# Attention logits as three half-height products, two heads in the two row halves of TensorE

## The chip, the cores and the metric

The kernel runs on one core of a Trainium2 chip. The metric is device time in microseconds from the first to the last instruction of the program on that core. Three runs of the kernel before gave 1956.97, 1957.89 and 1959.04 us; their median is 1957.89 us.

## The reference: what is computed

The input `x` is one sequence of 2048 positions of width 1024. It is normalised and multiplied by one wide input matrix, which yields the queries, keys and values of two attention mixers, gate paths and merge gates. All of it is fp32.

- Mixer A: 8 query heads share 2 key/value heads, head width 64, and each position looks at the 128 positions on either side of it. Each head has a sink logit.
- Mixer B: three groups of 8 heads, head width 64. Each group is a windowed attention on every first, fourth or sixteenth position, with 64 neighbours on either side. The groups are combined by their softmax denominators.

What the change touches is the step from the queries and keys to the logits:

```python
qa = head_rms_norm(qa.reshape(bsz, S, A_Q_HEADS, HEAD_DIM), q_norm_a[layer]) * scale
ka = head_rms_norm(ka.reshape(bsz, S, A_KV_HEADS, HEAD_DIM), k_norm_a[layer])
...
scores = jnp.einsum('bnqkgd,bnmkd->bkgnqm', qb, kw).astype(jnp.float32)
...
logits = jnp.where(valid, scores + bias, NEG_INF)
```

After the mixers, both outputs are gated, projected, merged by sigmoid gates, projected once more and added to `x`.

## The kernel before, in words

**Split numbers.** Matmuls run on fp16 operands. An fp32 value is stored as a high fp16 part and a low fp16 part (the rest), and a product is summed from several matmuls of parts into one fp32 accumulator. A projection uses three: high by high, high by low, low by high.

**Stages.** A first stage loads, normalises, transposes and splits `x` into `XH` and `XL`. The attention stage works through 14 units: 2 units of mixer A (4 query heads and their one key/value head each) and 12 of mixer B (a pair of heads of one group each). A last stage does the merge gates, the branch projections and the output projection.

**A unit.** A unit's positions are cut into 16 subsets of 128 positions, handled two at a time by class `Pair`, so there are 8 pairs for each unit. `Pair.matmuls` (line 651) projects a subset's queries, keys and values into a PSUM tile `pj`. `Pair.plan` then queues the steps `square`, `stats`, `newton`, `scale`, `gain`, `hi`, `lo`, `swap` and `turn`: the head norms on VectorE and GpSimd, and the split into the fp16 tile `spl`. `hi` (line 728, ScalarE) writes the high parts, `lo` (line 732, VectorE) the low parts. In `spl` a head's high part of 64 columns lies beside its low part, so that one head fills a block of 128 columns. `swap` (line 737, GpSimd) writes a further block for each key head, with low and high exchanged. `turn` (line 745) issues one DMA transpose for each subset from the SP queue; it gives the tile `kq`, six blocks of 128 rows by 128 positions. The rows of a block are the high and the low part of one head.

**An item.** Class `Item` holds one block of 128 queries and two heads: 256 items in all. `logits` (line 805) multiplies the query block with each key block, once as it is and once with its halves exchanged, so two matmuls of 128 rows give all four products of parts. An item has up to three key blocks in A (12 matmuls for two heads), two in B's first two groups (8) and one in the third (4). The logits stand in PSUM tiles `s` from a pool of three (`s_p`): an A item takes two tiles, one for each head, and a B item takes one tile with both heads beside each other. `maxima` (line 820, VectorE) adds the bias and takes the maximum, `exps` (line 828) and `hi` (line 833) run on ScalarE, `lo` (line 837) on VectorE, `turn` (line 843) transposes the probabilities by DMA into `pt`, and `values` (line 854) multiplies them with the values on TensorE.

**Order.** The order on every engine is written out by the kernel: `at(t, f)` puts a step on a heap of due times, and `until` calls what is due between the projections' matmuls. The offsets in `NORM` and `LAGS` set how long after its pair or item a step is issued. A step's matmuls are issued in one piece, so an item's logits stand as one burst between projection matmuls (lines 308 and 651) or matmuls of line 854. Waits between engines come from the tiles that the steps share.

Of the kernel before, what the change touches and what calls it, by code (L numbers as in the profile page):

```python
# [21 lines left out]
F32 = mybir.dt.float32  # L22
F16 = mybir.dt.float16
I32 = mybir.dt.int32
AF = mybir.ActivationFunctionType
OP = mybir.AluOpType
# [8 lines left out]
HD = 64  # L35
# [76 lines left out]
def block_kernel(tc, x, w_units, w_gate, w_mrg, w_brn, w_out, w_bra, gain, qkg, sink, bias_a, bias_b, b_merge, out):  # L112
    nc = tc.nc
    V = nc.vector
    A = nc.scalar
    G = nc.gpsimd
    T = nc.tensor
# [171 lines left out]
    s_p = main.enter_context(tc.tile_pool(name="sp", bufs=3, space=PSUM))  # L289
# [222 lines left out]
    def scale_time(t):  # L512
        return X_CH[0] + X_CH[1] * t
# [6 lines left out]
    for t in range(NT):  # L520
        b = X_SQ[0] + X_SQ[1] * t if t < 4 else X_SQ[2] + X_SQ[3] * (t - 4)
# [4 lines left out]
        b = scale_time(t)  # L526
        at(b, x_scale, t)
        for h in range(2):
            b = scale_time(t) + X_CH[2] + X_CH[5] * h
# [8 lines left out]
    for c in range(3):  # L538
        b = X_G[c]
# [34 lines left out]
    wk = main.enter_context(tc.tile_pool(name="wk", bufs=2, reuse_waits="tile"))  # L574
# [59 lines left out]
    class Pair:  # L634
# [7 lines left out]
        def matmuls(self, i):  # L642
            un, (r, c) = self.un, self.subsets[i]
            self.ps[i] = ps = pj_p.tile([128, 512], F32, name="pj")
            out = []
            for a, b, aligned in ((0, 128, True), (128, 384, False)) if un.shift else ((0, 384, True),):
                h, lo = subset(0, un.g, r, c, aligned), subset(1, un.g, r, c, aligned)
                k = 0
                for ch in range(NCH):
                    for lhs, rhs in ((h, un.wh), (h, un.wl), (lo, un.wh)):  # L650
                        out.append(lambda lhs=lhs, rhs=rhs, ch=ch, a=a, b=b, k=k: T.matmul(  # L651
                            ps[:, a:b], lhsT=lhs[:, ch, :], rhs=rhs[:, ch, a:b], start=(k == 0), stop=(k == 23)))
                        k += 1
            return out
# [38 lines left out]

        def square(self):
            n = 2 * self.nh * HD
            self.sp = wk.tile([128, 2, 6, 2, HD], F16, name="spl")
            self.sq = self.sp[:].rearrange("p a b c d -> p (a b c d)").bitcast(F32)
            A.activation(self.sq[:, :n], self.rw[:, :n], AF.Square)

        def stats(self):  # L700
# [23 lines left out]
        def hi(self):  # L724

            n = 2 * self.nh
            self.q = self.rw[:, :n * HD].rearrange("p (s h e) -> p s h e", s=2, e=HD)
            A.activation(self.sp[:, :, :self.nh, 0, :], self.q, AF.Copy)  # L728

        def lo(self):  # L730
            sp, nh = self.sp, self.nh
            V.tensor_tensor(sp[:, :, :nh, 1, :], self.q, sp[:, :, :nh, 0, :], OP.subtract)  # L732

        def swap(self):
            sp, nh, nq = self.sp, self.nh, self.un.nq
            for i in range(2):
                G.tensor_copy(sp[:, i, nh:, :, :], sp[:, i, nq:nh, ::-1, :])  # L737

        def turn(self):
            for i, s in enumerate(self.subsets):  # L740
                if self.un.shift and s[1] == 0:
                    kq = wk.tile([128, 6, 128], F16, name="kq0", bufs=3)
                else:
                    kq = wk.tile([128, 6, 128], F16, name="kq", bufs=KQ_BUFS)
                nc.sync.dma_start_transpose(out=kq[:], in_=self.sp[:, i].rearrange("p a b c -> p (a b c)"))
                self.un.kq[s] = kq


    class Item:
# [40 lines left out]
        def logits(self):  # L790
            un = self.un
            q = un.kq[(self.r, self.i)]
            if un.kind == "A":
                self.sv = [s_p.tile([128, 512], F32, name="s")[:, :self.W] for _ in range(2)]
            else:
                t = s_p.tile([128, 512], F32, name="s")
                self.sv = [t[:, self.W * j:self.W * j + self.W] for j in range(2)]
            for j in range(2):
                h = self.h0 + j
                kh = 0 if un.kind == "A" else h  # L800
                o = 0
                for s, k0, k1 in self.keys:
                    kt = un.kq[s]
                    for v in range(2):
                        T.matmul(self.sv[j][:, o:o + k1 - k0], lhsT=q[:, h, :],  # L805
                                 rhs=kt[:, un.nq + kh + v * un.nk, k0:k1], start=(v == 0), stop=(v == 1))
                    o += k1 - k0

        def stat(self, j):
            un = self.un  # L810
# [251 lines left out]
    for u in range(NU + 1):  # L1062
        t = 8 * u
# [8 lines left out]
    for c, u, slots in FILLS:  # L1072
# [4 lines left out]
        t = 8 * u  # L1077
# [5 lines left out]
    for k in range(8):  # L1083
        u = 3 + k
        t = 8 * u
# [10 lines left out]
    un, nxt = None, 0.0  # L1096
    t = 0
    while t < NPAIR or heap or any(k >= t for k in fill):
        u, j = divmod(t, 8)
        steps = [(f, args) for f, *args in fill.pop(t, [])]  # L1100
        if u < NU:
            if j == 0:
                un = Unit(u)
# [127 lines left out]
    def split(hi, lo, v, scale):  # L1231
        return (lambda: A.activation(hi, v, AF.Copy, scale=scale[:]),
                lambda: V.scalar_tensor_tensor(lo, v, scale[:], hi, OP.mult, OP.subtract))
# [211 lines left out]
    t = clock[0]  # L1445
# [120 lines left out]
    t = clock[0]  # L1566
# [7 lines left out]
    for k, (i, q) in enumerate(steps):  # L1574
# [3 lines left out]
        p = (i // 2, q % 2)  # L1578
# [168 lines left out]
```

## Time and profile before

| | us |
|---|---|
| median of three runs | 1957.89 (1956.97 to 1959.04) |
| span of the profiled execution | 1958.6 |
| TensorE busy | 1935.7 (17606 matmuls) |
| weight loads busy | 1392.0 |
| VectorE busy | 1377.4 |
| ScalarE busy | 1059.8 |
| GpSimd busy | 956.0 |
| line 805, logits, summed busy time | 150.7 (2016 matmuls) |

The profile lists instructions by line, engine, operation and tile. PE is TensorE's matmul row and PEld its weight loads, DVE is VectorE, ACT ScalarE, POOL GpSimd and SP the engine that issues the DMAs. A row's form, such as `128*128 128x128 f16`, gives the weights' rows and columns, then the output. A matmul's record lasts from its start to its modelled end, and records overlap: the price of a matmul in a full stream is the distance to the next start, not the length of its record. In groups by line, the time behind `|` is busy time and the mean of one in ns, and the time behind the second `|` is the idle time of the engine before them with its releaser. In waits, the three numbers are the total in us, the number of times and the longest.

### The profile page before, as it was taken

To read this page: it belongs to the slowest core of one execution; us is meant where nothing else is said; L and a number is where in the kernel's file an instruction comes from. 1 tells how busy PE (TensorE), PEld (TensorE's weight loads), DVE (VectorE), ACT (ScalarE), POOL (GpSimd) and SP (SyncE) were. 2 spreads that over 40 slices of the span, in tenths; PEclk is the share of its full clock that TensorE was granted. 3 is DMA by queue.
4 is the path that set the end of the run, shared out by engine and by line. 5 is a ranking of instruction groups with operands and counts; after the bars stand their busy time and mean duration, and the time that the engine had idled before them with its cause. 6 is when DMAs were issued, how large, how long until landed. Compare 5 with 4: busy or idle time off the path is not lost.

```text
span 1958.6 us, 48091 instructions
## 1 busy us (share of the span) xinstructions
PE 1935.7 (99%) x17606; PEld 1392.0 (71%) x17606; DVE 1377.4 (70%) x3604; ACT 1059.8 (54%) x2415; POOL 956.0 (49%) x2440
## 2 busy tenths in 40 slices
PE   8999999999999999999999999999999999999999
PEld 5567896677788898888989889899544444444444
DVE  6668777888768776667876878767776757876312
ACT  7457656776565566565666655656534545432100
POOL 4254556455546656647566676656511210232533
PEclk8999999999999999999999999999999999999999
DMA  6239987797848596677777776755822346788763
GB/s 250 81 81 168 194 150 159 141 187 141 177 101 184 118 185 126 125 148 164 152 132 154 135 169 126 143 118 118 187 81 85 106 165 195 218 241 268 252 228 145
DMA packets 589773, 308.46 MB, mean 157 GB/s; under 512 B 458080, under 2 KB 527328, under 8 KB 588256
## 3 DMA queue, kind: packets, MB, share of 16 engines
q1 hardware_dynamic: 589536, 305.39, 67.0%
q8 instruction: 137, 2.24, 0.5%
q14 instruction: 100, 0.82, 0.1%
HBM read 129.91 MB, written 65.27 MB: 100 GB/s over the span
## 4 chain that ended last, share of the span: by engine, by line
PE 80%; DVE 6%; POOL 6%; issue 4%; ACT 2%; DMA 2%; SPq 0%; POOLq 0%; DVEq 0%; ACTq 0%
PE pj L651 32%; PE pj L308 14%; PE fps L308 13%; PE fps L1614 7%; PE fps L1409 5%; PE s L805 4%; PE pv L854 4%; POOL rs_t L270 1%; DVE rw L715 1%; POOL rs_t L271 1%; DVE qss L703 1%; POOL rs_t L272 1%; POOL rw L722 1%; POOL rs_y L273 1%; PE pt L916 1%
## 5 line engine op out<-in xcount | busy, mean ns | idle before, releaser
L651 PE MATMUL pj<-wl,XH 128*128 128x128 f16 (+2 forms) x2816 | 715.2, 268 | 0.0
L651 PE MATMUL pj<-wh,XH 128*128 128x128 f16 (+2 forms) x2816 | 708.7, 268 | 4.0 <-DVE vt L691 4.0
L651 PE MATMUL pj<-wh,XL 128*128 128x128 f16 (+2 forms) x2816 | 711.6, 269 | 0.0
L651 PEld LDWEIGHTS <-XH 128*128 128x128 f16 x5632 | 574.6, 113 | 64.7 <-issue 5.8
L651 PEld LDWEIGHTS <-XL 128*128 128x128 f16 x2816 | 318.1, 113 | 26.7 <-issue 0.5
L820 DVE CUSTOM_DVE_ANT_0 pr<-s,b,ubuf 128x256 f32<-128x256 f32 (+3 forms) x512 | 218.6, 464 | 48.6 <-PE s L805 47.0
L270 POOL TENSOR_TENSOR rs_t<-rs_y 128x8 f32<-128x8 f32 (+2 forms) x345 | 105.4, 306 | 207.5 <-DVE rs_y L261 142.7
L837 DVE SCALAR_TENSOR_TENSOR p<-pr,p 128x512 f16<-128x512 f32 (+2 forms) x256 | 185.0, 723 | 21.6 <-ACT p L833 21.1
L308 PEld LDWEIGHTS <-wh 128*128 128x128 f16 x960 | 93.7, 98 | 111.0 <-issue 1.5
L715 DVE TENSOR_TENSOR rw<-rw,qr 128x512 f32<-128x512 f32 (+1 forms) x112 | 111.6, 997 | 86.7 <-POOL vt L678 58.4
L722 POOL TENSOR_TENSOR rw<-rw,g 128x128 f32<-128x128 f32 (+1 forms) x224 | 131.1, 605 | 78.1 <-DVE rw L715 62.1
L833 ACT ACTIVATE p<-pr 128x512 f16<-128x512 f32 (+2 forms) x256 | 159.5, 623 | 7.1 <-issue 0.3
L670 ACT ACTIVATE rw<-pj 128x256 f32<-128x256 f32 (+1 forms) x224 | 86.5, 386 | 134.3 <-PE pj L651 133.4
L737 POOL COPY spl<-spl 128x256 f16<-128x256 f16 (+1 forms) x224 | 93.7, 448 | 127.2 <-DVE spl L732 125.7
L308 PE MATMUL fps<-Y,wh 128*128 128x512 f16 x512 | 152.2, 379 | 0.0
L805 PE MATMUL s<-kq 128*128 128x128 f16 (+1 forms) x1856 | 147.3, 218 | 1.5 <-DMA kq<-spl 1.4
L805 PEld LDWEIGHTS <-kq 128*128 128x128 f16 x2016 | 129.8, 98 | 25.1 <-issue 2.0
L308 PE MATMUL pj<-XH,gh 128*128 128x512 f16 x384 | 145.5, 379 | 0.0
L308 PE MATMUL pj<-XH,gl 128*128 128x512 f16 x384 | 145.5, 379 | 0.0
L308 PE MATMUL pj<-XL,gh 128*128 128x512 f16 x384 | 145.5, 379 | 0.0
L1614 PE MATMUL fps<-wt,M 128*128 128x512 f16 (+1 forms) x684 | 145.2, 375 | 0.0
L728 ACT ACTIVATE spl<-rw 128x512 f16<-128x512 f32 (+1 forms) x112 | 72.1, 644 | 126.2 <-POOL vt L678 87.0
(241 smaller groups left out, 3702.2 us busy)
## 6 DMA issues: line engine op xcount, KB each, us to landing
wraw<-in_w_units_dram SPq DMA_DIRECT2D x56, 384.0 KB, 4.6
mtd<-mm SPq DMA_DIRECT2D x56, 256.0 KB, 3.7
M<-mtd SPq DMA_DIRECT2D x8, 1792.0 KB, 9.5
mgd<-fg SPq DMA_DIRECT2D x39, 256.0 KB, 2.1
zd<-z SPq DMA_DIRECT2D x128, 66.0 KB, 1.9
zz<-zd SPq DMA_DIRECT2D x64, 132.0 KB, 2.9
xt<-in_x_dram SPq DMA_DIRECT2D x16, 512.0 KB, 8.9
gtd<-yo SPq DMA_DIRECT2D x32, 256.0 KB, 2.7
```

The lines of the kernel that those rows point to most:

```text
L270: G.tensor_tensor(tv, yv, yv, OP.mult)
L308: out.append(lambda w=w, xx=xx, ch=ch, i=i: T.matmul(ps[:], lhsT=w[:, ch, c0:c0 + 128], rhs=xx[:, ch, ts], start=(i == 0), stop=(i == n - 1)))
L651: out.append(lambda lhs=lhs, rhs=rhs, ch=ch, a=a, b=b, k=k: T.matmul(ps[:, a:b], lhsT=lhs[:, ch, :], rhs=rhs[:, ch, a:b], start=(k == 0), ...
L715: V.tensor_tensor(q, q, self.rr[:, :n].unsqueeze(2).to_broadcast([128, n, HD]), OP.mult)
L722: G.tensor_tensor(q[:, i, :un.nq, :], q[:, i, :un.nq, :], g, OP.mult)
L737: G.tensor_copy(sp[:, i, nh:, :, :], sp[:, i, nq:nh, ::-1, :])
L805: T.matmul(self.sv[j][:, o:o + k1 - k0], lhsT=q[:, h, :], rhs=kt[:, un.nq + kh + v * un.nk, k0:k1], start=(v == 0), stop=(v == 1))
L820: V.tensor_tensor_reduce(out=self.pv[:, j, self.p0:self.p0 + W], in0=self.sv[j], in1=un.bias[:, self.h0 + j, self.b0:self.b0 + W], scale=I ...
L833: A.activation(self.sp[:, :128 * n], self.pr, AF.Copy, scale=PSC)
L837: V.scalar_tensor_tensor(self.sp[:, 128 * n:], self.pr, PSC, self.sp[:, :128 * n], OP.mult, OP.subtract)
L1409: mm.append(lambda ch=ch, k=k, w=w, i=i: T.matmul(ps[:], lhsT=weight(bl, ch)[w], rhs=xblock(x, ch)[k], start=(i == 0), stop=(i == 11)))
L1614: mm.append(lambda ch=ch, k=k, w=w, i=i: T.matmul(ps[:, :cols.stop - cols.start], lhsT=m[:, a, ch, k, :], rhs=wt[w][:, b, ch, cols], start ...
```

## The change

`spl` and `kq` get another layout, and `logits` another set of products.

- `hi` and `lo` write all high parts of a subset first and then all low parts. A block of 128 columns now holds two heads, 64 columns each, of one kind of part. After the transpose, one head lies in rows 0 to 63 and its partner in rows 64 to 127.
- In B a subset has four blocks (queries high, keys high, queries low, keys low), so the transpose moves four instead of six, and `swap` does nothing. In A there are six blocks, and `swap` copies the single key head next to itself, so that it lies in both halves.
- `logits` makes three products for each head and key block, high by high, high by low and low by high; the product of the two low parts is no longer made. Each is a matmul of 64 rows. The two heads of an item alternate, head 0 in rows 0 to 63 and head 1 in rows 64 to 127.
- Every item, B's too, takes two tiles `s`, one for each head. The pool still has three.

An item's burst has 18 matmuls in A (12 at the ends of the sequence), 12 in B's first two groups and 6 in the third.

```diff
         def square(self):
             n = 2 * self.nh * HD
-            self.sp = wk.tile([128, 2, 6, 2, HD], F16, name="spl")
-            self.sq = self.sp[:].rearrange("p a b c d -> p (a b c d)").bitcast(F32)
+            w = self.nw = 4 if self.un.kind == "B" else 6
+            sp = wk.tile([128, 2 * 2 * 6 * HD], F16, name="spl")
+            self.sp = sp[:, :4 * w * HD].rearrange("p (a b c d) -> p a b c d", a=2, b=2, d=HD)
+            self.sq = sp[:].bitcast(F32)
...
-            A.activation(self.sp[:, :, :self.nh, 0, :], self.q, AF.Copy)
+            A.activation(self.sp[:, :, 0, :self.nh, :], self.q, AF.Copy)
...
-            V.tensor_tensor(sp[:, :, :nh, 1, :], self.q, sp[:, :, :nh, 0, :], OP.subtract)
+            V.tensor_tensor(sp[:, :, 1, :nh, :], self.q, sp[:, :, 0, :nh, :], OP.subtract)
 
         def swap(self):
-            sp, nh, nq = self.sp, self.nh, self.un.nq
-            for i in range(2):
-                G.tensor_copy(sp[:, i, nh:, :, :], sp[:, i, nq:nh, ::-1, :])
+            if self.nw > self.nh:
+                for i in range(2):
+                    G.tensor_copy(self.sp[:, i, :, 5, :], self.sp[:, i, :, 4, :])
...
-                nc.sync.dma_start_transpose(out=kq[:], in_=self.sp[:, i].rearrange("p a b c -> p (a b c)"))
+                nc.sync.dma_start_transpose(out=kq[:, :self.nw, :], in_=self.sp[:, i].rearrange("p a b c -> p (a b c)"))
...
         def logits(self):
             un = self.un
             q = un.kq[(self.r, self.i)]
-            if un.kind == "A":
-                self.sv = [s_p.tile([128, 512], F32, name="s")[:, :self.W] for _ in range(2)]
-            else:
-                t = s_p.tile([128, 512], F32, name="s")
-                self.sv = [t[:, self.W * j:self.W * j + self.W] for j in range(2)]
-            for j in range(2):
-                h = self.h0 + j
-                kh = 0 if un.kind == "A" else h
-                o = 0
-                for s, k0, k1 in self.keys:
-                    kt = un.kq[s]
-                    for v in range(2):
-                        T.matmul(self.sv[j][:, o:o + k1 - k0], lhsT=q[:, h, :],
-                                 rhs=kt[:, un.nq + kh + v * un.nk, k0:k1], start=(v == 0), stop=(v == 1))
-                    o += k1 - k0
+            self.sv = [s_p.tile([128, 512], F32, name="s")[:, :self.W] for _ in range(2)]
+            nb = 3 if un.kind == "A" else 2
+            o = 0
+            for s, k0, k1 in self.keys:
+                kt = un.kq[s]
+                for i, (a, b) in enumerate(((0, 0), (0, 1), (1, 0))):
+                    for j in range(2):
+                        rows = slice(64 * j, 64 * j + 64)
+                        T.matmul(self.sv[j][:, o:o + k1 - k0], lhsT=q[rows, nb * a + (self.h0 + j) // 2, :],
+                                 rhs=kt[rows, nb * b + nb - 1, k0:k1], start=(i == 0), stop=(i == 2))
+                o += k1 - k0
```

## The prediction

> **What bounds the kernel.** I read the page's busy shares, slices and chain, then TensorE's waits, its rows by form, and the order of time around single bursts.
>
> ```profile
> span 1958.6 us, 48091 instructions
> PE 1935.7 (99%) x17606; PEld 1392.0 (71%) x17606; DVE 1377.4 (70%) x3604; ACT 1059.8 (54%) x2415; POOL 956.0 (49%) x2440
> ...
> PE   8999999999999999999999999999999999999999
> ...
> PEclk8999999999999999999999999999999999999999
> ...
> PE 80%; DVE 6%; POOL 6%; issue 4%; ACT 2%; DMA 2%; SPq 0%; POOLq 0%; DVEq 0%; ACTq 0%
> ```
>
> TensorE is busy in every slice after the first, at a full clock, and holds 80% of the chain that ended last. A busy share alone could hide small stalls, so TensorE's waits come next.
>
> ```profile
> PE s L468 <- DVE xt L462: 6.4, 4, 4.7
> PE pj L651 <- DVE vt L691: 4.0, 4, 2.4
> PE pt L194 <- DVE yo L920: 3.0, 1, 3.0
> PE s L805 <- DMA kq<-spl: 1.4, 3, 0.8
> ```
>
> These are the four longest; nothing else keeps TensorE waiting for more than about 1 us in total. So TensorE's stream of slots is the time: a slot that is added is added to the end, and work taken from another engine gives nothing. The logits that the change rewrites all lie in the attention stage:
>
> ```profile
> 110.00:1410.00 1300.00, 1290.96 (x14443) 1080.78 (x14442) 988.22 (x2886) 807.04 (x1987) 767.09 (x2226) 1.00 0.75 148
> ```
> ```profile
> 110.00:1410.00 1300.00, 150.70 (x2016) 129.84 (x2016) 1.00 0.75 148
> ```
>
> The first row is the whole stage (span, then busy time of TensorE, weight load, VectorE, ScalarE, GpSimd); the second is line 805 alone, with all its 2016 matmuls and 2016 weight loads.
>
> **What the logits cost now.** Records overlap, so their busy time isn't their price; the price is the distance from one start to the next.
>
> ```profile
> 400.65 0.83 PE L805 MATMUL s<-kq 128*128 128x128 f16 x12
> 401.32 0.33 PE L651 MATMUL pj<-wl,XH 128*128 128x384 f16 x1
> ...
> 402.27 0.70 PE L854 MATMUL pv<-vt,pt 128*128 128x65 f16 x18
> 402.81 0.32 PE L651 MATMUL pj<-wh,XH 128*128 128x384 f16 x1
> ```
> ```profile
> L805 PE MATMUL s<-kq 128*128 128x128 f16 x1776 | 139.5, 219 | 1.5 <-DMA kq<-spl 1.4
> L805 PE MATMUL s<-kq,kq 128*128 128x128 f16 x80 | 8.9, 220 | 0.0
> L805 PE MATMUL s<-kq,kq 128*128 128x64 f16 x80 | 7.8, 193 | 0.0
> L805 PE MATMUL s<-kq 128*128 128x64 f16 x80 | 7.8, 193 | 0.0
> ```
>
> Twelve logit matmuls of 128 columns take 401.32 - 400.65 = 0.67 us, 56 ns each. Eighteen matmuls of 64 or 65 columns of line 854, each with a new 128x128 weight load, take 0.54 us, 30 ns each: that is the price of a short matmul, and also the fastest rate at which this trace shows weight loads being fed. So now: (1776 + 80) x 56 + 160 x 30 ns = 108.7 us.
>
> **Part 1: three products of half height for two of full height.** Per key block and head there were two matmuls; there are three, 1.5 times as many: 3024, of which 2784 have 128 columns and 240 have 64. All records of before say 128*128, so no row shows a 64-row matmul, nor whether two of them in the two row halves run at once. Bounds:
> - Wholly side by side, a pair takes one slot: half of (2784 x 56 + 240 x 30) = 81.6 us, a gain of 27.1.
> - One after the other, each takes its slot: 163.1 us, a loss of 54.4.
> - Side by side, but fed by weight loads at the 30 ns of line 854: 3024 x 30 = 90.7 us, a gain of 18.0.
>
> I take the third, -18.0: the two heads alternate in the diff, each with its own tile `s` and its own rows, and a weight load precedes each matmul, so the nearest row is the one that is paced by weight loads. The Trainium skill ("TensorE: Matmul & The Clock Gate", Part 3) says that matmuls whose operands lie in different row groups run concurrently, and gives 3.07 times for four tiles of 32 rows with 512 columns; by that alone, at its best of two for one, the time would be 1958.6 - 27.1 = 1931.5. No row here shows it.
>
> **Part 2: the change of height.** Each burst of logits now stands between matmuls of 128 rows, so TensorE goes from 128 rows to 64 and back once for each item. ScalarE's line 833 runs once for each item:
>
> ```profile
> L833 ACT ACTIVATE p<-pr 128x512 f16<-128x512 f32 (+2 forms) x256 | 159.5, 623 | 7.1 <-issue 0.3
> ```
>
> 256 items are 512 changes of height. Neighbours of unlike width and line follow each other now without a gap, but the height never changes, so the price of a change isn't shown. Lower end 0; below nothing is excluded, since a change of height computes nothing and takes nothing away. For the upper end:
>
> ```profile
> 805.62 0.38 PE L308 MATMUL pj<-XH,gl 128*128 128x512 f16 x1
> 805.62 0.43 PEld L805 LDWEIGHTS <-kq 128*128 128x128 f16 x4
> ...
> 805.84 0.39 PE L805 MATMUL s<-kq 128*128 128x128 f16 x4
> ...
> 806.06 0.38 PE L308 MATMUL pj<-XH,gh 128*128 128x512 f16 x1
> ```
> ```profile
> L805 PEld LDWEIGHTS <-kq x2016: 95/98/98, 112.8 to 1409.1; 128*128 128x128 f16 x184
> ```
>
> A logit matmul lasts 219 ns while its successor starts after 56: a tail of 163 ns is hidden under the next. The 512-column one has the same tail (0.38 against 0.22 us). Weight loads are pulled ahead too: the first of the four starts at 805.62, its matmul at 805.84. If a change of height takes both overlaps away, it costs 163 + 98 = 261 ns. Ends 0 and 261, no row nearer to either; I take the middle, 130 ns: 512 x 0.130 = +66.6 us (0 to 133.6).
>
> The Trainium skill ("TensorEngine Tiling (Array Packing)", Tiling Modes) says that changing the tiling mode, not just the tile, drains TensorE. It gives no price. If the drain is the 163 ns tail, it costs 83.5 us instead of 66.6, and the sum below would be 2026. No row of before has a change of mode to hold against it.
>
> Against the 18.0 us of part 1, the point from which the change loses is 18.0 / 512 = 35 ns a change (27.1 / 512 = 53 ns at the best pairing).
>
> **Part 3: two tiles `s` for each B item.** The pool has three. B items used one, and now use two, so the second head's first matmul must wait until VectorE has read the first head of the item before. It is in TensorE's order, so every projection behind it waits as well. I laid each burst against VectorE's line 820 of the tile that it would reuse. Only four of the bursts come too early, the worst here:
>
> ```profile
> 1113.20 0.91 PE L805 MATMUL s<-kq 128*128 128x128 f16 x8
> 1118.27 0.61 PE L805 MATMUL s<-kq 128*128 128x128 f16 x8
> ```
> ```profile
> 1120.59 0.47 DVE L820 CUSTOM_DVE_ANT_0 pr<-s,b,ubuf 128x256 f32<-128x256 f32 x1
> ```
>
> The burst of 1118.27 would wait for the read of the item of 1113.20, until 1121.06: 2.8 us. The next is 1.2 us, and all four together 4.1 us. TensorE will itself be later if part 2 holds, which lengthens VectorE's room: I take +2, with ends 0 and 4.
>
> **Part 4: edits off the path.** The POOL copy is dropped for B, and its transposes have four blocks instead of six.
>
> ```profile
> L737 POOL COPY spl<-spl 128x256 f16<-128x256 f16 (+1 forms) x224 | 93.7, 448 | 127.2 <-DVE spl L732 125.7
> ```
>
> 192 of 224 copies go, 192 x 448 ns = 86 us of GpSimd, which is 49% busy and which TensorE never waits for. So 0; at the most the 1.4 us that TensorE waits for `kq` goes. The same instructions of ScalarE and VectorE write `spl` at other addresses: 0. The first head's logits are finished only with the burst, under 0.3 us later; TensorE's waits name none of the steps behind them (neither VectorE's line 820 nor the transposes `pt`): 0. DMA issues keep their number and order on SP.
>
> **Sum.** 1958.6 - 18.0 + 66.6 + 2 = 2009.2, so 2009 us. The profiled span is 0.7 us over the median of the runs, 1957.89, which is within their spread (1956.97 to 1959.04).
>
> **Rivals.**
> - *The change of height is almost free.* Speaks for it: matmuls of unlike width and line follow each other without a gap in the rows above. Against it: a tail of 163 ns that only identical heights have been seen to hide. It decides below 35 ns a change. Time: 1958.6 - 18.0 = 1940.6, down to 1931.5 with full pairing and 1930.1 without the `kq` wait. This is the case on the other side.
> - *The halves do not run at once.* For it: every slot in the trace is one matmul's own, and a half-height one could wait for its neighbour in the same way. Against it: separate rows and separate output tiles leave it no cause. Time: 1958.6 + 54.4 = 2013 with free changes of height, 2080 with 130 ns each.
> - *Little changes.* Price of a change near 35 ns, so that parts 1 and 2 cancel: 1955 to 1962.
>
> **How the numbers follow.** My forecast (side by side, a change of height that costs clearly over 35 ns) has 0.58, the free change 0.22, the halves one after the other 0.16, cancelling 0.04. Hence faster 0.22, same 0.04, slower 0.74; about 0.2%, 3.9 us, is what a measurement of this kernel tells from no change. The likeliest case has its own range, 1965 to 2078 (1958.6 - 18.0 + 4 + 133.6). The full range reaches into the free-change case, 1936, and to 2070 above, where only near-full overlap loss or serial halves with dear changes lie beyond: about 2 in 10 are left out.
>
> **What the profile after would show.** Part 1: inside a burst, two starts within some 60 ns mean side by side; starts 56 ns apart mean one after the other. Part 2: a burst of 6 or 12 should begin later after the matmul ahead of it than that one's width explains, and the projection behind the burst likewise; without such gaps part 2 is wrong. Part 3: waits of line 803 for VectorE's line 818, of a few us in all. Part 4: GpSimd about 86 us less busy. I am wrong if the gap is under 35 ns, or if TensorE's rate elsewhere changes (the projections at 128, 256 and 384 columns, line 854 at 30 ns).

## The result

The changed kernel takes 1979.88 us (1979.35 to 1981.32), the kernel before 1957.99 us beside it. The ratio is 1.0112, with a 95% interval from 1.0098 to 1.0127: slower by 21.9 us, where 51 were forecast. The direction was right, and the size was less than half of the forecast.

The page of the changed kernel, where the first four lines answer to those shown of before:

```profile
span 1979.5 us, 49754 instructions
PE 1963.7 (99%) x18614; PEld 1351.0 (68%) x18614; DVE 1376.8 (70%) x3604; ACT 1061.1 (54%) x2415; POOL 875.6 (44%) x2248
...
PEclk9999999999999999999999999999999999999999
...
PE 93%; DVE 3%; POOL 2%; issue 1%; ACT 1%; DMA 0%; SPq 0%; DVEq 0%; POOLq 0%; ACTq 0%
```

TensorE has 1008 more matmuls, and it is still what sets the end. GpSimd is 80 us less busy and nothing came of it. TensorE's share of the chain rose from 80% to 93%, and its idle time fell: span less busy time was 1958.6 - 1935.7 = 22.9 us and is 1979.5 - 1963.7 = 15.8 us. Its rates outside the bursts stayed as they were: 56, 109, 163 and 216 ns from start to start at 128, 256, 384 and 512 columns, and 29 at the 64 and 65 columns of `values`. Its longest waits after:

```profile
PE s L468 <- DVE xt L462: 5.2, 4, 3.7
PE pj L651 <- DVE vt L691: 2.2, 2, 1.8
PE s L803 <- DVE nmB L818: 1.4, 1, 1.4
```

The third is the wait of part 3, for the second tile `s`: one time, 1.4 us. Now one burst of an A item in the order of time (start, length, engine), with weight loads:

```profile
400.77 0.33 PE L651 MATMUL pj<-wh,XL 128*128 128x384 f16 x1
...
400.93 0.33 PE L651 MATMUL pj<-wh,XH 128*128 128x384 f16 x1
401.19 0.51 PEld L803 LDWEIGHTS <-kq 64*128 64x128 f16 x18 [0.32 <-issue]
401.19 0.68 PE L803 MATMUL s<-kq 64*128 64x128 f16 x18
401.79 0.10 PEld L651 LDWEIGHTS <-XH 128*128 128x128 f16 x1
401.80 0.34 PE L651 MATMUL pj<-wl,XH 128*128 128x384 f16 x1
401.81 0.10 PEld L651 LDWEIGHTS <-XL 128*128 128x128 f16 x1
401.97 0.33 PE L651 MATMUL pj<-wh,XL 128*128 128x384 f16 x1
```

The reader is to see three things.

- *The pairs.* Eighteen matmuls take 401.80 - 401.19 = 0.61 us, where the 12 of before took 0.67. Two matmuls share one slot of 56 ns: 9 x 56 = 504 ns, and the rest is the gap behind the burst and the slower first pair.
- *The gap ahead.* The matmul at 400.77 has its next start after 0.16 us, the one at 400.93 after 0.26, and the weight loads of the burst start only with it, at 401.19. Over all 256 bursts the gap ahead is 96 ns, whatever stands ahead of it (projection of 128 to 512 columns).
- *The gap behind.* From the last start of a burst to the next matmul 148 ns pass, where the second of a pair else leaves 53: 95 ns more. The weights of the next matmul are loaded at 401.79, just ahead of it, not pulled ahead.

Two smaller pieces belong to it. The first pair of a burst takes 66 or 67 ns instead of 56. And the first matmul behind a burst holds up the second. How much goes by the length of the first one's own weight load, which nothing covers. Above, the load took 0.10 us and the second matmul started 0.17 us after the first, where 0.16 is usual; here is another burst:

```profile
411.54 0.33 PE L651 MATMUL pj<-wh,XL 128*128 128x384 f16 x1
411.80 0.50 PEld L803 LDWEIGHTS <-kq 64*128 64x128 f16 x18 [0.27 <-issue]
411.80 0.68 PE L803 MATMUL s<-kq 64*128 64x128 f16 x18
412.40 0.21 PEld L651 LDWEIGHTS <-XH 128*128 128x128 f16 x2
412.41 0.39 PE L651 MATMUL pj<-wh,XH 128*128 128x384 f16 x1
412.63 0.33 PE L651 MATMUL pj<-wl,XH 128*128 128x384 f16 x1
```

Here the projection reads every sixteenth position of `XH`, the load took 144 ns, and 0.22 us pass, 59 ns too many. Sorted by the first matmul's load, the hold-up is 10 ns at loads of 95 to 96 ns, 28 at 112 to 116 (every fourth position) and 57 at 140 to 148 (every sixteenth): each time the load less some 85 ns. It is 23 ns on average over before. The gap behind, 148 or 149 ns, is the same beside short and long loads, so the load isn't what makes the gap.

So a change of height there and back costs 96 + 95 + 11 + 23 = 225 ns, and 256 of them, summed before rounding, 57.5 us. The pairs gain the full 27.1 us (108.7 to 81.6). Summed from the start of the last matmul ahead of each burst to the second behind it, less those two slots, the bursts took 114.8 us before and take 141.3 us: +26.6, of which -27.1 + 57.5 = +30.4, and -3.8 is waits inside the bursts that went. Outside, TensorE's other waits fell by some 6 us. That leaves the 20.9 us between the two spans.

The listed waits of TensorE, all lines together, fell from 19.3 to 12.6 us: the 3.0 us for `yo` and the 1.4 for `kq` are gone, those for `xt`, `vt` and `gh` are 3.7 shorter together, and the new one for `s` is 1.4. That is 6.7 us of the 9.5 or so that went inside and outside the bursts; the rest is stalls that the list doesn't name.

### The profile page after: what moved, and what is told of

Read it like the earlier page. It is cut to its first block, busy times and chain, and to the rows that moved or that the text cites. A ratio compares the mean times of both kernels' runs of the same rounds, so it can differ in the third digit from the quotient of the medians.

```text
span 1979.5 us, 49754 instructions
## 1 busy us (share of the span) xinstructions
PE 1963.7 (99%) x18614; PEld 1351.0 (68%) x18614; DVE 1376.8 (70%) x3604; ACT 1061.1 (54%) x2415; POOL 875.6 (44%) x2248
## 4 chain that ended last, share of the span: by engine, by line
PE 93%; DVE 3%; POOL 2%; issue 1%; ACT 1%; DMA 0%; SPq 0%; DVEq 0%; POOLq 0%; ACTq 0%
PE pj L651 42%; PE pj L308 15%; PE fps L308 13%; PE fps L1612 7%; PE s L803 5%; PE fps L1407 5%; PE pv L852 4%; PE pt L914 1%; PE s L468 1%; POOL rs_t L270 0%; DMA xt<-in_x_dram 0%; DVE rw L717 0%; POOL rs_t L271 0%; POOL rs_t L272 0%; DVE qss L705 0%
## 5 line engine op out<-in xcount | busy, mean ns | idle before, releaser
L270 POOL TENSOR_TENSOR rs_t<-rs_y 128x8 f32<-128x8 f32 (+2 forms) x345 | 101.2, 293 | 395.0 <-DVE rs_y L261 292.7
L852 PEld LDWEIGHTS <-pt 128*128 128x128 f16 x3024 | 122.2, 97 | 22.1 <-DMA pt<-p 0.3
L180 POOL TENSOR_TENSOR wraw<-wraw,gn 128x768 f32<-128x768 f32 (+1 forms) x80 | 113.4, 1425 | 43.2 <-DMA wraw<-in_w_mrg_dram 29.5
L852 PE MATMUL pv<-vt,pt 128*128 128x65 f16 (+1 forms) x2784 | 131.7, 193 | 0.0
L803 PEld LDWEIGHTS <-kq 64*128 64x128 f16 x3024 | 82.9, 94 | 69.7 <-issue 65.8
```

What stands on the lines that cost most here:

```text
L180: G.tensor_tensor(v, v, gn[:, c0:c0 + 2].unsqueeze(2).to_broadcast([128, 2, n]), OP.mult)
L270: G.tensor_tensor(tv, yv, yv, OP.mult)
L803: T.matmul(self.sv[j][:, o:o + k1 - k0], lhsT=q[rows, nb * a + (self.h0 + j) // 2, :], rhs=kt[rows, nb * b + nb - 1, k0:k1], start=(i == 0 ...
L852: T.matmul(self.po[:, j, :w], lhsT=p[:, n * j + s, :], rhs=un.v[key][:, vh, c0:c0 + w], start=(k == 0 and s == 0), stop=(k == 2 and s == n ...
```

## The experiments

Every run is given as its ratio to runs of the kernel before on the same chip, and differences are taken between ratios, since the kernel before itself stood between 1958.0 and 1960.4 us beside them. The whole change is 1.0112 by this measure.

**Is it the height? A full-height matmul between the key blocks, and a half-height one as its control.** The result of the further matmul is overwritten by the block's own products.

```diff
                 kt = un.kq[s]
+                if o:
+                    T.matmul(self.sv[0][:, o:o + 64], lhsT=q[:, 0, :], rhs=kt[:, 0, 0:64], start=True, stop=True)
```

> The changed kernel with one more matmul of 128 rows and 64 columns ahead of each further key block of an item (248 in all: 136 items with two key blocks, 56 with three), in the columns of head 0 that the block's own products then overwrite. Each takes TensorE from 64 rows to 128 and back once more. Theory (it is the change of height that costs, 224 ns there and back: 96 ns before a burst, 95 after it, 11 in its first pair and 22 in the first matmul behind it): 248 x (0.224 + 0.029) = +63 us, 2043 us. Rival (the gaps around a burst come from something else that a burst brings, such as its new weights, new tiles or its waits): only the slots of 30 to 56 ns, +7 to +14 us, 1987 to 1994 us.

The control has `q[0:64, 0, :]` and `kt[0:64, 0, 0:64]` in the same line.

> The control to the run before: the same 248 further matmuls in the same places with the same columns, but of 64 rows (rows 0 to 63), so that the height does not change. Theory (height): only the slots, 29 to 56 ns each, +7 to +14 us, 1987 to 1994 us. Rival (any further matmul of other operands opens the gaps): as the run before, about +63 us, 2043 us.

Measured: 2037.15 us with full height, ratio 1.0395 (1.0379 to 1.0411), which is 55 us over the change; 1988.51 us with half height, 1.0141 (1.0122 to 1.0161), 6 us over it. One item of the first run, then one of the second:

```profile
438.46 0.33 PE L651 MATMUL pj<-wh,XL 128*128 128x384 f16 x1
438.71 0.34 PE L805 MATMUL s<-kq 64*128 64x128 f16 x6
438.99 0.20 PE L801 MATMUL s<-kq 128*128 128x64 f16 x1
439.12 0.34 PE L805 MATMUL s<-kq 64*128 64x128 f16 x6
439.40 0.20 PE L801 MATMUL s<-kq 128*128 128x64 f16 x1
439.54 0.34 PE L805 MATMUL s<-kq 64*128 64x128 f16 x6
439.81 0.39 PE L651 MATMUL pj<-wh,XH 128*128 128x384 f16 x1
```
```profile
416.31 0.33 PE L651 MATMUL pj<-wh,XL 128*128 128x384 f16 x1
416.57 0.34 PE L805 MATMUL s<-kq 64*128 64x128 f16 x6
416.75 0.19 PE L801 MATMUL s<-kq 64*128 64x64 f16 x1
416.75 0.38 PE L805 MATMUL s<-kq 64*128 64x128 f16 x7
416.94 0.19 PE L801 MATMUL s<-kq 64*128 64x64 f16 x1
416.97 0.33 PE L805 MATMUL s<-kq 64*128 64x128 f16 x5
417.23 0.38 PE L651 MATMUL pj<-wh,XH 128*128 128x384 f16 x1
```

The +55 us is under the 63 expected, and the bursts alone grew by 58. The burst with two full-height matmuls takes 439.81 - 438.71 = 1.10 us, the one with two half-height matmuls 0.66, and without either it is 0.61. Summed over the trace, a full-height matmul costs 235 ns and a half-height one 26. That it is the change of height, and not the further matmul with its own weights, is shown. The Trainium skill ("TensorEngine Tiling (Array Packing)", Tiling Modes) says that a change of the tiling mode drains TensorE, and that a change of tile does not. The two runs agree; what it costs here is 112 ns a change on average, less than the tail of 163 ns of a matmul's record. In the second item, two matmuls start at 416.75: a row of two matmuls running at once.

**Do the heads have to alternate?**

```diff
-                for i, (a, b) in enumerate(((0, 0), (0, 1), (1, 0))):
-                    for j in range(2):
+                for j in range(2):
+                    for i, (a, b) in enumerate(((0, 0), (0, 1), (1, 0))):
```

> The changed kernel with the heads no longer alternating: for each key block, the three products of head 0, then the three of head 1. Matmuls, bytes and changes of height stay as they are. Theory (two matmuls run at once only where neighbours in the order lie in the two row halves): all but the one pair at each change of head fall apart, slots of 56 ns each instead of 56 ns a pair. The logits go from 81.6 us towards 163.1 us; about two matmuls in six still pair (the last of head 0 with the first of head 1, and the last of head 1 with the first of the next key block), so between +50 and +82 us on 1980: 2030 to 2061 us. Rival 1 (TensorE looks ahead and pairs anyway): 1980 us. Rival 2 (a weight load is pulled ahead only beside a matmul in the other half, so that 94 ns of load stand bare between matmuls of one half): about 150 ns a matmul, 3024 x 150 = 454 us instead of 81.6, over 2250 us.

Measured: 1982.53 us, 1.0115 (1.0099 to 1.0130), the time of the change. The theory fell and rival 1 held. A burst of 12:

```profile
1264.12 0.33 PE L651 MATMUL pj<-wh,XH 128*128 128x384 f16 x1
1264.38 0.52 PE L803 MATMUL s<-kq 64*128 64x128 f16 x12
1264.83 0.38 PE L651 MATMUL pj<-wl,XH 128*128 128x384 f16 x1
```

It takes 0.45 us, 448 ns at the median against 441 when they alternate. If matmuls started strictly in order, each group of three would pair only its last with the first of the next, and 12 would take at least nine slots before the gap behind, 504 ns, and some 600 with it. So a matmul in one half starts ahead of earlier ones that wait for the other half. The Trainium skill ("TensorE: Matmul & The Clock Gate", Part 3) says that matmuls start and end in program order, and that only weight loads are pulled ahead; this run differs from it, and the measurement decides. The records don't name the half, so in this run the overtaking is worked out from the length of the burst; in the next one it can be read start by start.

How far it goes was asked with the next kernel, two items in a burst, by placing all of head 0's matmuls of a burst ahead of all of head 1's.

```diff
+            for j in range(2):
+                rows = slice(64 * j, 64 * j + 64)
+                for it in (self,) if un.kind == "A" else self.pair:
+                    q = un.kq[(it.r, it.i)]
...
```

> The kernel with two B items in a burst (1974 us), with head 0's matmuls of a burst all first and head 1's all behind them: 12 and 12 in B's first two groups, 9 and 9 in A, instead of alternating one by one. The run with the heads apart by three matmuls paired all the same, 448 ns for a burst of 12. Theory now (each row half runs its own stream of matmuls, and a matmul of one half overtakes waiting ones of the other): if it looks 12 ahead, the burst of 24 stays at about 697 ns and the time at 1974 us. Rival (it overtakes only a few places): a burst of 24 towards 24 x 56 + 95 = 1440 ns, of 18 towards 1100, of 12 towards 770, in all 64 x 0.74 + 56 x 0.5 + 40 x 0.33 = +88 us at the most: up to 2062 us, and a value between tells how far it looks.

Measured: 2013.88 us, 1.0281 (1.0265 to 1.0296), against 1.0076 of the kernel it is made from. It lies between theory and rival.

```profile
401.61 0.97 PE L818 MATMUL s<-kq 64*128 64x128 f16 x18
402.51 0.34 PE L651 MATMUL pj<-wl,XH 128*128 128x384 f16 x1
...
508.75 0.64 PE L818 MATMUL s<-kq 64*128 64x128 f16 x12
509.32 0.39 PE L308 MATMUL pj<-XH,gh 128*128 128x512 f16 x1
...
609.06 1.31 PE L818 MATMUL s<-kq 64*128 64x128 f16 x24
610.30 0.39 PE L308 MATMUL pj<-XH,gh 128*128 128x512 f16 x1
```

These bursts of 18, 12 and 24 take 0.90, 0.57 and 1.24 us. One after the other, with 106 ns for the gap behind and the first pair, they would take 1.11, 0.78 and 1.45. The saving is 0.21 us each time, close to four slots of 56 ns, however long the burst is (0.12 to 0.20 in the 40 bursts that hold matmuls of 64 columns). The single starts in the trace agree. In the burst of 12 above they fall into two rows: 0, 67, 123, 179, 235 and 290 ns, and 131, 198, 254, 310, 365 and 421, each with a first step of 67 and then steps of some 56. The second row begins when three matmuls of the first are still to start, and four of its matmuls run beside the first row. That holds in all 120 bursts whose matmuls have 128 columns, whether 6, 9 or 12 of the first head come first: a matmul overtook three waiting ones of the other half, and no more.

**Is the price paid for each burst? Two B items in one burst.** The first item's steps up to its transpose are put off to the second's times, and two tiles `s` serve both.

```diff
+                elif mate is not None:
+                    for it in (mate, self):
+                        it.pair = (mate, self)
+                        at(drain(s + d), getattr(it, f.__name__))
...
+            elif self is self.pair[0]:
+                t = [s_p.tile([128, 512], F32, name="s") for _ in range(2)]
```

> The changed kernel with the logits of two B items in one burst: the first item's logits and its steps up to the transpose are put off to the second item's times, and the two items share the two tiles, head 0 of both in one and head 1 of both in the other. Matmuls and pairing stay, but there are 160 bursts instead of 256. Theory (each burst pays 224 ns for going to 64 rows and back): 96 x 0.224 = -21.5 us, 1958 us, about where the kernel before stands. Rival (the price hangs on the number of pairs, not of bursts): 1980 us. Second rival (the first item's steps, half a pair later, now make TensorE wait for the transposed probabilities): a gain under 21 us, with waits of line 854's counterpart for the transposes in the list of TensorE's waits.

Measured: 1974.16 us, 1.0076 (1.0059 to 1.0092), 7 us under the change. The price was paid back in full in the bursts: 117.3 us for all 160 against 141.3 for 256, -24. TensorE's waits took most of it: those listed, all lines together, are 26.1 us where the change has 12.6. The longest of that run:

```profile
PE pv L863 <- DMA pt<-p: 9.6, 9, 2.4
PE s L468 <- DVE xt L462: 6.3, 3, 3.9
PE pj L651 <- DVE vt L691: 4.8, 4, 1.8
```

The first wasn't there: the probabilities of the item that was put off come too late for its values. Two runs put off the values as well.

```diff
-LV = {'A': 1.111, 'B': 1.829}
+LV = {'A': 1.111, 'B': 2.1}
```

> The kernel with two B items in a burst, with the B items' values put off by 0.27 of a pair (about 3 us). In the run before, TensorE's price for the bursts fell as expected (141.3 to 117.3 us) but the time by 5.7 us only, with nine waits of 9.6 us in all for the transposed probabilities. Theory (those waits took the gain): they go, 1974 - 10 = 1964 us, and less than that if what feeds TensorE behind them, the queue of the stores and of the next unit, is late instead. Rival (the waits are not what took it): 1974 us.

Measured: 1991.20 us, 1.0164 (1.0147 to 1.0181): slower. The waits for `pt` were gone (0.6 us), but the late values held the tiles `vt`. The waits of GpSimd and TensorE in that run:

```profile
POOL vt L678 <- PE pv L863: 108.4, 33, 12.9
...
PE pj L651 <- DVE vt L691: 11.6, 9, 3.4
```

GpSimd waits in its order for a free `vt` (69 us in the run before), with the norms behind it, and TensorE's wait for `vt` rose from 4.8 to 11.6 us. That the norms pass the delay on is read from these waits and not shown by a run of its own. The second run put the values off by 0.12 of a pair (`'B': 1.95`) and had 11 buffers of `vt`; it changes both at once, so it doesn't tell their shares.

> The kernel with two B items in a burst, with the B items' values put off by 0.12 of a pair instead of 0.27, and one more buffer for the value tiles vt (11 instead of 10). The run with 0.27 lost its waits for the transposed probabilities but became slower (1991 us), with GpSimd waiting 108 us instead of 69 for a vt that the late values still held. Theory (two items in a burst are worth 21 us where nothing that feeds TensorE is late; a smaller delay and a freer vt give part of it back): 1962 to 1970 us, with waits for the probabilities under 5 us. Rival (a delay of any size is passed on through vt and the norms): 1975 us or more.

Measured: 1969.69 us, 1.0056 (1.0038 to 1.0075), 11 us under the change, with 3.1 us of waits for `pt`. It is at the upper end of what was expected, and still slower than the kernel before.

**Where it is lost: A alone and B alone.** A branch by `un.kind` keeps layout, products and tiles of before for the other units.

```diff
+            if un.kind != "A":
+                return self.logits_full()
             self.sv = [s_p.tile([128, 512], F32, name="s")[:, :self.W] for _ in range(2)]
```

> The change in the two A units alone (64 of 256 items); the B units keep layout, products and tiles of the kernel before. Theory (224 ns for each burst, a gain of 56 ns for each key block and two heads): an inner A item has three key blocks, 224 - 168 = +56 ns, 56 of them; an end item has two, +112 ns, 8 of them; together +4.0 us, 0.2% on the kernel before. Rival (the first runs' price is B's, with its small bursts, and A with its long bursts gains): -1 us or less, faster than the kernel before.

> The change in the twelve B units alone (192 of 256 items); A keeps the kernel before. Theory: 128 items with two key blocks at 224 - 112 = +112 ns and 64 with one at 224 - 56 = +168 ns, +25.1 us, less up to 7 us of TensorE's waits that go when it is slower: +18 to +25 us. This and the run before together should give the whole change's +22. Rival (the parts do not add, because waits decide): a sum outside 17 to 29 us.

Measured: A alone 1960.68 us, 1.0001 (0.9992 to 1.0009), no difference; B alone 1977.50 us, 1.0083 (1.0070 to 1.0096), 16 us slower, a little under its range. The interval of A alone reaches from -1.6 to +1.8 us: the +4 expected did not show in the time, and a gain isn't shown either.

In the bursts, the prices came out and the parts add. A's bursts took 41.1 us before and 44.8 both in the run of A alone and in the whole change, +3.7. B's took some 73.6 before, 96.6 in B alone and 96.4 in the whole. What A's bursts lost was made up elsewhere in that profile, 2.4 us of it by waits inside B's bursts; that is little, since the 17 runs of the kernel before beside it range from 1957.3 to 1965.7 us.

In the time, the two parts sum to 16.5 us, just under the 17 to 29 given as the bounds. Their intervals (1.7 and 2.5 us to either side) reach across that line, so whether they add in the time stays open. The order by size holds: nearly all is lost in B, whose bursts have fewer key blocks.

**The parts costed at little or nothing.** Two tiles `s` in the kernel before:

```diff
-                t = s_p.tile([128, 512], F32, name="s")
-                self.sv = [t[:, self.W * j:self.W * j + self.W] for j in range(2)]
+            self.sv = [s_p.tile([128, 512], F32, name="s")[:, :self.W] for _ in range(2)]
```

> The kernel before with one part of the change alone: B items take two tiles s, one for each head, from the same pool of three; layout, products and heights stay as before. Theory (four bursts come before VectorE has read the tile, 4.1 us in all): 0 to +4 us on the kernel before. Rival (the fewer tiles in flight cost several us by pushing the projections behind the bursts as well): +5 us or more.

Measured: 1958.20 us, 1.0000 (0.9990 to 1.0010). TensorE's waits for the tile appear, and others shrink, 18.9 us of listed waits in all against 19.3:

```profile
PE s L801 <- DVE nmB L816: 2.3, 2, 1.7
```

And the changed kernel with B's blocks and copies put back:

```diff
-            w = self.nw = 4 if self.un.kind == "B" else 6
+            w = self.nw = 6
...
+            for i in range(2):
+                G.tensor_copy(self.sp[:, i, :, nh:, :], self.sp[:, i, :, nq:nh, :])
```

> The changed kernel with the part that was costed at nothing undone: B's transposes move six blocks again and GpSimd copies again (192 more copies, into blocks that nothing reads), while the products stay 64 rows high. Theory (off the path; TensorE's idle time fell from 18.6 to 11.5 us because a slower TensorE leaves the other engines more room): 1980 us, within 2. Rival (the shorter transposes and the missing copies are what took 7 us of TensorE's waits away): +7 us, 1987 us.

Measured: 1982.04 us, 1.0118 (1.0103 to 1.0133), the time of the change. The shorter transposes and the missing copies gave nothing.

## Why the prediction was right and wrong

- *What bounds the kernel: right in the main.* TensorE's slots set the time before and after, and the 80 us taken from GpSimd gave nothing. But "a slot that is added is added to the end" didn't hold: 30.4 us of slots were added, and 20.9 arrived at the end.
- *Part 1, half height: side by side right, the limit by weight loads wrong.* The halves run at once, and a pair takes one slot of 56 ns, so the gain was 27.1 us, the upper end, not 18.0. The row chosen for it failed: line 854's 30 ns was taken for the fastest rate of weight loads. In the bursts, one of 64 rows is fed every 28 ns, and every 14.5 where pairs of 64 columns follow each other at 29 ns a pair. Whether loads of 128 rows are held to 30 ns isn't shown. 9.1 us of the error.
- *Part 2, change of height: mechanism right, size too large.* 112 ns a change on average instead of 130, 57.5 us instead of 66.6. The upper end was right in kind: both overlaps go, the tail of the matmul ahead and the early weight load, but the tail isn't waited out in full (96 and 95 ns, not 163), and the bare load shows only as a hold-up of the second matmul (10 to 57 ns). The 130 was the middle of 0 to 261 with no row behind it, so that it came within 18 ns of the price is luck. 9.1 us of the error.
- *Part 3: right.* One wait of 1.4 us; alone it makes no difference that can be measured.
- *Part 4: right.* Putting the blocks and copies back changed nothing.
- *What the sum left out.* It kept TensorE's waits as they were, and they fell: the spans differ by 20.9 us, the slots by 57.5 - 27.1 = 30.4, so 9.5 us of waits inside and outside the bursts went, where +2 stood in the sum. 11.5 us of the error, the largest share. The prediction saw for part 3 that a later TensorE gives VectorE more room, and left this out for the waits that were there already. That TensorE's work, longer by 30 us, leaves the others more room is the reading that fits, and no run shows it by itself; that it was the shorter transposes is excluded by the run with six blocks. Which waits go in which run varies, and that is not settled.

So the step that failed is the sum: it took 18.0 us off where the pairs gave 27.1, put on 66.6 where the changes of height cost 57.5, and put on 2 for waits where 9.5 went. The values of parts 1 and 2 lay inside their ends, and 1980 us inside the stated range, but all three errors pointed one way: they make the 29.7 us between the forecast and the profiled span. The lower end of the likeliest case, 1965, isn't worked out in the prediction; by its own terms (27.1 off, 512 changes at 35 ns on) it would be 1949. Of the rivals, the free change of height falls (112 ns a change, not under 35). The halves one after the other fall too, since two matmuls share a slot. Cancelling, 1955 to 1962, falls by the time alone.

## What to carry to other kernels

Half-height matmuls in the two row halves do run at once here, but each burst of them paid 225 ns for going to 64 rows and back. For this kernel's products (three of half height for two of full height, 128 columns) a key block of two heads gains 56 ns, so a burst breaks even at four key blocks, and it has one to three. The run with two items in a burst agrees: its bursts with four key blocks of 128 columns take 776 ns to the next matmul, 882 with the gap ahead and the hold-up, where two bursts of 8 took 2 x 446 = 892 before. So count the changes of height, not the matmuls alone, and where an engine is slowed, take the waits that it has now into the sum: some of them may come off the price, as 9.5 us did here.

## What the runs showed that was not expected

- Matmuls in different row halves need not alternate in the order: three of one half and then three of the other pair as well as one by one (448 against 441 ns for 12). Beyond that, a matmul overtakes three waiting ones of the other half and no more, whether 6, 9 or 12 stand ahead of it, so four of the later half run beside the earlier half.
- The weight load behind a burst is bare, and it holds up the second matmul by its length less some 85 ns: a load of 95 to 96 ns adds 10, one of 140 to 148 from a source read at every sixteenth position adds 57.
- A half-height matmul that has no partner costs no more than a slot: the two further ones in a burst of A cost 0.05 us together.
